# Wider padded tiles in a two-block layer kernel: 576 columns in place of 542

## The chip, the cores and the metric

The kernel runs on one core of one Trainium2 chip. The metric is the device time of one execution in microseconds (us). The kernel before takes 1970.71 us, the median of 3 runs (1970.65 to 1971.37).

## The reference, cut to what matters

The input is a sequence of 512 tokens with 1024 channels. It passes through two blocks of two layers each.

Each layer of the first block normalizes, projects to 3584 channels and splits them into four mixers of 256 channels: (a) a gated 31-wide depthwise convolution with a layer norm, (b) a 3-wide gated convolution, (c) attention in a sliding window, (d) attention in a 2-D neighbourhood. Their gated outputs are joined and projected back.

```python
y_a = conformer_conv(...) * silu(a_z)          # 31-wide convolution over positions
y_b = short_gated_conv(...) * silu(b_z)        # 3-wide convolution
return x + einsum("bse,ed->bsd", concat([y_a, y_b, y_c, y_d]), w_out)
```

Each layer of the second block has a running mean over windows of 2, 4, 8 and 16 tokens, a latent attention with 8 heads, a linear recurrence after a 4-wide convolution, three gates that merge them, an output projection, and a feed-forward part of 4096 hidden channels:

```python
x = x + merged @ w_out
x = x + square(relu(rms_norm(x) @ w_ff1)) @ w_ff2
```

All of it is in 32-bit floats. The kernel multiplies in a split form: each operand is a high part plus a low part, and three products (high by high, high by low, low by high) are summed.

## The kernel before, in words

Activations lie with channels on the 128 partitions and the 512 tokens along the free dimension, so a tile of 128 channels is 128x512 floats, 2048 bytes in each partition. `gemm` (L158 on) makes one such output tile: it loads 512 KB of weights into `raw`, splits them into `whi` and `wlo` (`weights`, L136 to L144, `split`, L122 to L129), and `mm3` (L148 to L154) issues for each of the 8 input tiles three matmuls: `whi` with the high part (L152), `whi` with the low part (L153), `wlo` with the high part (L154). That is 24 matmuls of 128x512 for a tile; the loaded weights are the stationary operand, the activations are streamed.

The second block's layer ends with three stretches made of nothing but such tiles. The output projection (L878 on, `w_out_2`) streams the tiles `mh`, `ml`. Four quarters of the feed-forward part follow; each has 8 tiles with `w_ff1_2` (L894, streaming `hh`, `hl`) and 8 tiles with `w_ff2_2` (L904, streaming `fh`, `fl`). So each of these stretches has 192 matmuls. In the last quarter of the last layer the second product is done otherwise (from L923): there `fh` and `fl` are the stationary operand, the weights `wfh`, `wfl` are streamed, and each of 8 output tiles has 24 matmuls behind four transposes.

All buffers come from pools with a fixed number of slots under a tag. The tiles of one tag lie side by side in each partition, and the tags stand in the order of their first use. The pool `act` has, among others, the tags `hl` (32 slots: the split activations `xh`, `xl`, `hh`, `hl`, `yh`, `oh`, `wfh` and so on), `work` (8), `pad` (3), `hc` (2: the sums of the 31-wide convolution, later two tiles of `v`), `prob` (2), `gate` (16: `fh`, `fl`, `mh`, `ml`, the attention's `q`, `k`, `dq`, `dk`, `dv`, biases and gates) and `pth` (4: `pt`). In the program before, each slot's start is a multiple of 32 bytes, and the starts are these (bytes in each partition):

| tag | first slot at | from slot to slot | bytes of a tile |
|---|---|---|---|
| `raw`, `whi`, `wlo` (weights) | 27008, 35200, 47488 | 4096 | 4096 |
| `hl` | 76160 | 2048 | 2048 |
| `work` | 141696 | 2048 | 2048 |
| `pad` | 164992 | 2176 | 2168 |
| `hc` | 171520 | 2048 | 2048 |
| `prob` | 175616 | 5120 | 5120 |
| `gate` | 185856 | 2048 | 2048 |
| `pth` | 218624 | 2048 | 2048 |

The last byte in use is 226815; a partition has 229376. `c_ident`, the identity of the transposes, is at 18272, `ones_r` at 17760.

The tag `pad` serves the padded inputs of the convolutions (L483, L549), of the running means (L757, L766) and of the recurrence's convolution (L789), and three tiles without padding (`a2`, L810, and `gf`, L918, both cut to 512 columns). GpSimd writes the zeros at their ends. Only L485 writes up to the tile's end: `G.memset(pad[:, S + 15 :], 0.0)`. All others name their columns.

The order of the instructions on each engine is set ahead of time by the planner of the tile framework, which moves work within an engine's queue where its operands and slots allow; the waits follow from the tiles.

Of the kernel before, what the change touches and what calls it, by code (L numbers as in the profile page):

```python
# [9 lines left out]
F32 = mybir.dt.float32  # L10
# [6 lines left out]
P = 128  # L17
S = 512
# [39 lines left out]
def two_blocks(ctx: ExitStack, tc: tile.TileContext, g: dict):  # L58
# [5 lines left out]
    ap_ = ctx.enter_context(tc.tile_pool(name="act", bufs=1))  # L64
# [4 lines left out]
    def uniq(n):  # L69
        cnt[0] += 1  # L70
        return f"{n}_{cnt[0]}"

    def work(n="w", shape=(P, S), dt=F32):
        return ap_.tile(list(shape), dt, tag="work", name=uniq(n), bufs=WORK)
# [13 lines left out]
    def auxps(n="aux"):  # L88
        return ps.tile([P, S], F32, tag="t", name=uniq(n), bufs=2)
# [16 lines left out]
    def col(name, l, c):  # L106
        o, w = VCOL[name]
        o += l * w + c
        return vec[:, o : o + 1]
# [21 lines left out]
    def split_tile(src, scale=None, n="h"):  # L131
        hi, lo = hl(n + "h"), hl(n + "l")
        split(src, hi, lo, scale)
        return hi, lo
# [192 lines left out]
    def scaled(p, R, n="e", alloc=work):  # L327
        t = alloc(n)
        V.tensor_tensor(t, p, R, op=ALU.mult)  # L329
        return t  # L330
# [25 lines left out]
    def hcol(name, l, c):  # L356
        o, w = VCOL[name]
        o += l * w + c
        return hvec[:, o : o + 1]
# [26 lines left out]
    for l in range(DEPTH):  # L386
        def proj(c):
            return first.pop(c) if c in first else gemm(g["w_in"][l, c], xs)
# [72 lines left out]
        for c in range(2):  # L461
            t, r = ts[c], work("cqr")
            rope(t, cos, sin, r, acopy)
            cq.append(queries(r, hl, "cqx"))
        t = scaled(proj(CK), R, "ck")
# [8 lines left out]
        def tap(acc, pad, c, k):  # L474
            V.scalar_tensor_tensor(acc, pad[:, k : k + S], hcol("conv_a_w", l, c * 31 + k), acc,
                                   op0=ALU.mult, op1=ALU.add)

        for c in range(2):
            v = scaled(proj(AV + c), R, "av")
            t = work("avt")  # L480
            A.activation(t, v, AF.Tanh, scale=0.5)
            u = scaled(proj(AU + c), R, "au")
            pad = ap_.tile([P, S + 30], F32, tag="pad", name=uniq("pad"), bufs=3)  # L483
            G.memset(pad[:, :15], 0.0)
            G.memset(pad[:, S + 15 :], 0.0)  # L485
            V.scalar_tensor_tensor(pad[:, 15 : S + 15], t, 1.0, u, op0=ALU.add, op1=ALU.mult)
            acc = ap_.tile([P, S], F32, tag="hc", name=uniq("hc"), bufs=2)
            V.tensor_scalar(acc, pad[:, 0:S], hcol("conv_a_w", l, c * 31), col("conv_a_b", l, c),
                            op0=ALU.mult, op1=ALU.add)
            for k in range(1, 31):  # L490
                taps.append(lambda acc=acc, pad=pad, c=c, k=k: tap(acc, pad, c, k))
            hc.append(acc)
# [53 lines left out]
        def conv_b(c):  # L546
            xb = scaled(proj(BX + c), R, "bx")
            cb = scaled(proj(BC + c), R, "bc")
            pad = ap_.tile([P, S + 30], F32, tag="pad", name=uniq("padb"), bufs=3)  # L549
            G.memset(pad[:, :1], 0.0)  # L550
            G.memset(pad[:, S + 1 : S + 2], 0.0)
            V.tensor_tensor(pad[:, 1 : S + 1], cb, xb, op=ALU.mult)
            return pad
# [36 lines left out]
        def finish_a(c):  # L590
# [10 lines left out]
            "dv": lambda c: values(scaled_tiles(proj(DV + c), "dv"), gate, "dv"),  # L601
            "zd": lambda c: gated(proj(DZ + c), R),
            "xb": conv_b, "hb": gate_b, "yb": finish_b, "ya": finish_a, "ln": lambda c: layer_norm(),
        }
        order = ["zc0", "bias0", "dq0", "zc1", "dk0", "dv0", "xb0", "hb0", "yb0", "zd0", "bias1", "dq1", "dk1", "dv1", "ln0",
# [67 lines left out]
    for l in range(DEPTH):  # L673
# [13 lines left out]
        for c in range(2):  # L687
            t = scaled(proj(5 + c), R, "kl")
# [4 lines left out]
        for c in range(3):  # L693
            t = scaled(proj(2 + c), R, "ql")
# [59 lines left out]
        ypool = {}  # L754

        def pool(c):
            pu = ap_.tile([P, S + 30], F32, tag="pad", name=uniq("padp"), bufs=3)  # L757
            G.memset(pu[:, :16], 0.0)
            V.tensor_tensor(pu[:, 16 : S + 16], proj(c), R, op=ALU.mult)
            cur = pu  # L760
            mixed = work("mixed")

            w = 1
            wins = (2, 4) if c == 0 else (8, 16)
            while w < wins[1]:
                nxt = ap_.tile([P, S + 30], F32, tag="pad", name=uniq("padd"), bufs=3)  # L766
                G.memset(nxt[:, :16], 0.0)
                V.tensor_tensor(nxt[:, 16 : S + 16], cur[:, 16 : S + 16], cur[:, 16 - w : S + 16 - w], op=ALU.add)
                cur = nxt
                w *= 2  # L770
                for j in range(2):
                    if w == wins[j]:
                        r0 = 64 * j
                        V.tensor_tensor(mixed[r0 : r0 + 64, 0:16], cur[r0 : r0 + 64, 16:32], invc[r0 : r0 + 64, c, :],
                                        op=ALU.mult)
                        V.tensor_scalar(mixed[r0 : r0 + 64, 16:], cur[r0 : r0 + 64, 32 : S + 16], 1.0 / w, None,
                                        op0=ALU.mult)
            V.tensor_tensor(mixed, mixed, pu[:, 16 : S + 16], op=ALU.subtract)
            p = auxps("pool")
            T.matmul(p, lhsT=bd["w_pool_grp_2", c], rhs=mixed, start=True, stop=True)  # L780
            t = work("yp")
            A.activation(t, p, AF.Copy, scale=col("pool_scale_2", l, c))
            ypool[c] = split_tile(t, None, "yp")
# [2 lines left out]
        ylru, lru = {}, {}  # L786

        def lru_in(c):
            pu = ap_.tile([P, S + 30], F32, tag="pad", name=uniq("padl"), bufs=3)  # L789
            G.memset(pu[:, :3], 0.0)  # L790
            V.tensor_tensor(pu[:, 3 : S + 3], proj(8 + c), R, op=ALU.mult)
            u = work("u")
            V.tensor_scalar(u, pu[:, 0:S], col("conv_w_2", l, c * 4), col("conv_b_2", l, c), op0=ALU.mult, op1=ALU.add)
            for k in range(1, 4):
                V.scalar_tensor_tensor(u, pu[:, k : k + S], col("conv_w_2", l, c * 4 + k), u, op0=ALU.mult, op1=ALU.add)
            p = auxps("ga")
            T.matmul(p, lhsT=bd["w_lru_a_2", c], rhs=u, start=True, stop=True)
            tr = work("tr")
            A.activation(tr, p, AF.Tanh, bias=hcol("b_lru_a_2", l, c), scale=0.5)
            p = auxps("gx")  # L800
            T.matmul(p, lhsT=bd["w_lru_x_2", c], rhs=u, start=True, stop=True)
            ti = work("ti")
            A.activation(ti, p, AF.Tanh, bias=hcol("b_lru_x_2", l, c), scale=0.5)
            V.scalar_tensor_tensor(ti, ti, 1.0, u, op0=ALU.add, op1=ALU.mult)

            V.tensor_scalar(tr, tr, 1.0, sp4[:, 2 * l + c : 2 * l + c + 1], op0=ALU.add, op1=ALU.mult)
            a = work("a")
            A.activation(a, tr, AF.Exp, scale=-1.0)
            A.activation(tr, tr, AF.Tanh)
            a2 = ap_.tile([P, S + 30], F32, tag="pad", name=uniq("a2"), bufs=3)[:, :S]  # L810
            A.activation(a2, a, AF.Square)
            V.scalar_tensor_tensor(a2, a2, 1.0, tr, op0=ALU.add, op1=ALU.mult)
            lru[c] = (a, a2, ti)
# [20 lines left out]
        def early_gate(m):  # L834
            tg1[m] = gate_of(1, m, gate)

        pieces = [(("pool", c), lambda c=c: pool(c)) for c in range(2)] + [(("lru", c), lambda c=c: lru_in(c)) for c in range(2)]
        pieces += [(("scan", 0), lru_scan)]
        pieces += [(("gate", m), lambda m=m: early_gate(m)) for m in range(KD)]
# [19 lines left out]
        for m in range(KD):  # L859
# [3 lines left out]
            for i, k0, ops_ in ((0, 0, ypool), (2, 6, ylru), (1, 2, yo)):  # L863
                p = mmps("br")
                mm3(p, [((h[:, k0 + k, :], lo[:, k0 + k, :]), ops_[k]) for k in range(len(ops_))])
                t = work("mgt")
# [24 lines left out]
        for qt in range(4):  # L891
            f = []
            for c in range(8):
                p = gemm(g["w_ff1_2"][l, 8 * qt + c], hs)  # L894
                t = work("relu")
# [7 lines left out]
            for m in range(KD):  # L903
                p = gemm(g["w_ff2_2"][l, qt, m], f)  # L904
                t = work("ff")
# [9 lines left out]

    gf = []
    for h in range(2):
        t = ap_.tile([P, S + 30], F32, tag="pad", name=uniq("gf"), bufs=3)[:, :S]  # L918
        nc.sync.dma_start(out=t, in_=g["g_final"][:, h * S : (h + 1) * S].to_broadcast([P, S]))
        gf.append(t)  # L920
    ss = small("ssh")
# [143 lines left out]
```

## Time and profile before

| | |
|---|---|
| median of 3 runs | 1970.71 us |
| the profiled execution | 1971.46 us |
| its span, from the first to the last instruction | 1969.6 us |
| TensorE busy | 1930.3 us, 98% of the span |
| VectorE, ScalarE, GpSimd busy | 1208.8, 839.6, 68.3 us |
| mean granted TensorE clock | 0.996 of full speed (2.4 GHz) |

The profiled execution is one more execution than those of the median. Matmuls are pipelined, so the duration that is shown for one (some 390 ns) is longer than the distance from its start to the start of the next.

### The profile page before, as it was taken

To read this page: it belongs to the slowest core of one execution; us is meant where nothing else is said; L and a number is where in the kernel's file an instruction comes from. 1 tells how busy PE (TensorE), PEld (TensorE's weight loads), DVE (VectorE), ACT (ScalarE), POOL (GpSimd) and SP (SyncE) were. 2 spreads that over 40 slices of the span, in tenths; PEclk is the share of its full clock that TensorE was granted. 3 is DMA by queue.
4 is the path that set the end of the run, shared out by engine and by line. 5 is a ranking of instruction groups with operands and counts; after the bars stand their busy time and mean duration, and the time that the engine had idled before them with its cause. 6 is when DMAs were issued, how large, how long until landed. Compare 5 with 4: busy or idle time off the path is not lost.

```text
span 1969.6 us, 23167 instructions
## 1 busy us (share of the span) xinstructions
PE 1930.3 (98%) x8866; PEld 1532.7 (78%) x8866; DVE 1208.8 (61%) x2127; ACT 839.6 (43%) x1391; POOL 68.3 (3%) x83
## 2 busy tenths in 40 slices
PE   7999999999999999999999999999999999999998
PEld 6777777777776778888888888766788888888886
DVE  8996678966787545565444446786455564444454
ACT  6565354663457633333232324367433333323242
POOL 0000110000200000020000001000000010000001
PEclk9999999999999999999999999999999999999999
DMA  5222222222212123233333333222222323323341
GB/s 191 75 94 84 86 97 75 85 85 66 84 50 79 65 75 97 97 96 93 91 95 96 97 96 97 83 62 83 65 86 97 97 95 91 96 94 97 96 128 43
DMA packets 53678, 175.21 MB, mean 89 GB/s; under 512 B 6208, under 2 KB 10176, under 8 KB 53568
## 3 DMA queue, kind: packets, MB, share of 16 engines
q1 hardware_dynamic: 53568, 173.74, 28.0%
q8 instruction: 70, 1.15, 0.2%
q14 instruction: 40, 0.33, 0.1%
HBM read 171.62 MB, written 2.10 MB: 88 GB/s over the span
## 4 chain that ended last, share of the span: by engine, by line
PE 72%; DVE 3%; ACT 2%; issue 1%; ACTq 0%; DVEq 0%
PE mm L152 20%; PE mm L154 19%; PE mm L153 19%; PE o L313 2%; PE sc L742 2%; PE br L154 1%; PE br L153 1%; PE br L152 1%; PE t L235 1%; PE last L154 1%; PE last L152 1%; PE last L153 1%; DVE wlo L126 1%; ACT p L284 0%; PE ss L169 0%
## 5 line engine op out<-in xcount | busy, mean ns | idle before, releaser
L125 ACT ACTIVATE whi<-raw 128x1024 fp32r<-128x1024 f32 (+2 forms) x314 | 321.4, 1025 | 779.6 <-PE mm L153 577.1
L126 DVE TENSOR_TENSOR wlo<-raw,whi 128x1024 fp32r<-128x1024 f32 (+2 forms) x314 | 369.1, 1176 | 168.1 <-ACT whi L125 168.1
L152 PE MATMUL mm<-xh,whi 128*128 128x512 f32 x992 | 397.8, 401 | 9.0 <-ACT whi L125 8.0
L154 PE MATMUL mm<-xh,wlo 128*128 128x512 f32 x992 | 392.7, 396 | 2.3 <-DVE wlo L126 2.2
L153 PE MATMUL mm<-xl,whi 128*128 128x512 f32 x992 | 394.3, 397 | 0.0
L152 PEld LDWEIGHTS mm<-xh,whi 128*128 128x128 f32 x992 | 187.6, 189 | 50.2 <-ACT whi L125 8.9
L154 PEld LDWEIGHTS mm<-xh,wlo 128*128 128x128 f32 x992 | 187.5, 189 | 43.4 <-DVE wlo L126 4.1
L153 PEld LDWEIGHTS mm<-xl,whi 128*128 128x128 f32 x992 | 187.8, 189 | 40.4 <-issue 4.3
L153 PE MATMUL mm<-hl,whi 128*128 128x512 f32 x512 | 199.5, 390 | 0.0
L152 PE MATMUL mm<-hh,whi 128*128 128x512 f32 x512 | 199.3, 389 | 0.0
L154 PE MATMUL mm<-hh,wlo 128*128 128x512 f32 x512 | 199.2, 389 | 0.0
L154 PE MATMUL mm<-fh,wlo 128*128 128x512 f32 x448 | 177.0, 395 | 0.0
L152 PE MATMUL mm<-fh,whi 128*128 128x512 f32 x448 | 176.9, 395 | 0.0
L153 PE MATMUL mm<-fl,whi 128*128 128x512 f32 x448 | 176.9, 395 | 0.0
L906 DVE TENSOR_TENSOR ff<-mm,rstd 128x512 f32<-128x512 f32 x56 | 38.8, 692 | 148.3 <-PE mm L154 148.3
L152 PEld LDWEIGHTS mm<-hh,whi 128*128 128x128 f32 x512 | 96.1, 188 | 20.1
L153 PEld LDWEIGHTS mm<-hl,whi 128*128 128x128 f32 x512 | 96.1, 188 | 19.9
L154 PEld LDWEIGHTS mm<-hh,wlo 128*128 128x128 f32 x512 | 96.1, 188 | 19.9
L329 DVE TENSOR_TENSOR lg<-mm,rstd 128x512 f32<-128x512 f32 x48 | 33.2, 691 | 124.3 <-PE mm L154 124.2
L154 PEld LDWEIGHTS mm<-fh,wlo 128*128 128x128 f32 x448 | 84.1, 188 | 20.4
L153 PEld LDWEIGHTS mm<-fl,whi 128*128 128x128 f32 x448 | 84.1, 188 | 20.4
L152 PEld LDWEIGHTS mm<-fh,whi 128*128 128x128 f32 x448 | 84.1, 188 | 20.4
(302 smaller groups left out, 2801.0 us busy)
## 6 DMA issues: line engine op xcount, KB each, us to landing
raw<-in_w_in SPq DMA_DIRECT2D x124, 512.0 KB, 3.3
raw<-in_w_ff SPq DMA_DIRECT2D x120, 512.0 KB, 3.6
raw<-in_w_out SPq DMA_DIRECT2D x32, 512.0 KB, 3.5
raw<-in_w_br SPq DMA_DIRECT2D x16, 512.0 KB, 3.6
raw<-in_w_last SPq DMA_DIRECT2D x8, 512.0 KB, 3.6
raw<-in_w_q SPq DMA_DIRECT2D x12, 192.0 KB, 2.3
x<-in_xT SPq DMA_DIRECT2D x8, 256.0 KB, 6.5
bends<-in_rpb SPq DMA_DIRECT2D x8, 256.0 KB, 4.4
```

What stands on the lines that cost most here:

```text
L125: A.activation(hi, src, AF.Copy)
L126: V.tensor_tensor(lo, src, hi.bitcast(F32), op=ALU.subtract)
L152: T.matmul(out, lhsT=wh, rhs=xh, start=(first and i == 0), stop=False)
L153: T.matmul(out, lhsT=wh, rhs=xl, start=False, stop=False)
L154: T.matmul(out, lhsT=wl, rhs=xh, start=False, stop=(last and i == n - 1))
L235: T.matmul(out, lhsT=in_, rhs=ident, is_transpose=True, start=True, stop=True)
L313: T.matmul(out[64 * j : 64 * j + 64, i * P : (i + 1) * P], lhsT=v(b), rhs=pts[j][:, (b - b0) * P : (b - b0 + 1) * P], start=(b == b0), sto ...
L329: V.tensor_tensor(t, p, R, op=ALU.mult)
L742: T.matmul(out, lhsT=q[h][:, i * P : (i + 1) * P], rhs=kt[h][:, b0 * P : b1 * P], start=True, stop=True)
L906: V.tensor_tensor(t, p, Rf2, op=ALU.mult)
```

## The change

Every tile of the tag `pad` becomes 576 columns wide in place of 542, in eight places of the code. No line is added or taken away. Each tile has 2304 bytes in place of 2168, and what comes behind the three slots in the partition begins further up. The slice `pad[:, S + 15 :]` of L485 now has 49 columns in place of 15.

```diff
-            pad = ap_.tile([P, S + 30], F32, tag="pad", name=uniq("pad"), bufs=3)
+            pad = ap_.tile([P, S + 64], F32, tag="pad", name=uniq("pad"), bufs=3)
             G.memset(pad[:, :15], 0.0)
             G.memset(pad[:, S + 15 :], 0.0)
...
-            pad = ap_.tile([P, S + 30], F32, tag="pad", name=uniq("padb"), bufs=3)
+            pad = ap_.tile([P, S + 64], F32, tag="pad", name=uniq("padb"), bufs=3)
...
-            pu = ap_.tile([P, S + 30], F32, tag="pad", name=uniq("padp"), bufs=3)
+            pu = ap_.tile([P, S + 64], F32, tag="pad", name=uniq("padp"), bufs=3)
...
-                nxt = ap_.tile([P, S + 30], F32, tag="pad", name=uniq("padd"), bufs=3)
+                nxt = ap_.tile([P, S + 64], F32, tag="pad", name=uniq("padd"), bufs=3)
...
-            a2 = ap_.tile([P, S + 30], F32, tag="pad", name=uniq("a2"), bufs=3)[:, :S]
+            a2 = ap_.tile([P, S + 64], F32, tag="pad", name=uniq("a2"), bufs=3)[:, :S]
...
-        t = ap_.tile([P, S + 30], F32, tag="pad", name=uniq("gf"), bufs=3)[:, :S]
+        t = ap_.tile([P, S + 64], F32, tag="pad", name=uniq("gf"), bufs=3)[:, :S]
```

(`padl`, L789, changes in the same way.)

## Rows read from the trace of the kernel before

**Rows 1.** The page, busy time, share of the span and instructions of two engines.
```profile
PE 1930.3 (98%) x8866; PEld 1532.7 (78%) x8866; DVE 1208.8 (61%) x2127; ACT 839.6 (43%) x1391; POOL 68.3 (3%) x83
PEclk9999999999999999999999999999999999999999
```
**Rows 2.** The page, chain that ended last: share of the span by engine.
```profile
PE 72%; DVE 3%; ACT 2%; issue 1%; ACTq 0%; DVEq 0%
```
**Rows 3.** Groups by line and shape, TensorE; columns: count, busy us, mean ns, idle before.
```profile
L152 PE MATMUL mm<-hh,whi 128*128 128x512 f32 x512 | 199.3, 389 | 0.0
L154 PE MATMUL mm<-hh,wlo 128*128 128x512 f32 x512 | 199.2, 389 | 0.0
L154 PE MATMUL mm<-fh,wlo 128*128 128x512 f32 x448 | 177.0, 395 | 0.0
L152 PE MATMUL mm<-fh,whi 128*128 128x512 f32 x448 | 176.9, 395 | 0.0
...
L152 PE MATMUL mm<-mh,whi 128*128 128x512 f32 x128 | 50.6, 395 | 0.0
...
L152 PE MATMUL last<-wfh,fh 128*128 128x512 f32 x64 | 25.9, 405 | 0.0
L154 PE MATMUL last<-wfh,fl 128*128 128x512 f32 x64 | 25.3, 395 | 0.0
...
L152 PE MATMUL br<-oh,whi 128*128 128x512 f32 x64 | 24.9, 389 | 0.0
```
**Rows 4.** Timeline of TensorE: starts (us) where one stretch gives way to the next.
```profile
840.63 0.40 PE L152 MATMUL mm<-mh,whi 128*128 128x512 f32 x1
...
885.43 0.39 PE L152 MATMUL mm<-hh,whi 128*128 128x512 f32 x1
...
975.58 0.39 PE L152 MATMUL mm<-hh,whi 128*128 128x512 f32 x1
...
1019.11 0.40 PE L152 MATMUL mm<-fh,whi 128*128 128x512 f32 x1
...
1063.90 0.39 PE L152 MATMUL mm<-hh,whi 128*128 128x512 f32 x1
```
**Rows 5.** Windows of ff1 and ff2: PE, PEld, DVE, ACT, POOL, clock, DMA, GB/s.
```profile
976.00:1018.00 42.00, 42.00 (x187) 34.74 (x186) 19.92 (x24) 15.89 (x22) 0.00 (x0) 1.00 0.31 94
1020.00:1062.00 42.00, 42.00 (x181) 33.79 (x180) 20.17 (x24) 8.76 (x10) 0.00 (x0) 1.00 0.28 88
```
**Rows 6.** Waits inside the same ff2 stretch: us in total, times, longest.
```profile
ACT whi L125 <- PE mm L153: 31.0, 8, 4.5
DVE ff L906 <- PE mm L154: 19.7, 7, 3.0
```
**Rows 7.** Groups by line and shape: score matmuls from two tags.
```profile
L437 PE MATMUL sc<-dk,dq 128*128 128x384 f32 x32 | 8.8, 345 | 0.0
L437 PE MATMUL sc<-ckx,cqx 128*128 128x384 f32 x32 | 8.4, 345 | 0.0
```
**Rows 8.** Groups by line and shape: matmuls on `ones_r`, `pt` and the values.
```profile
L313 PE MATMUL o<-pt,v 128*64 128x128 f32 x320 | 35.9, 286 | 2.5 <-ACT pt L309 2.2
L313 PE MATMUL o<-pt,cv 128*64 128x128 f32 x160 | 18.8, 288 | 0.4
L313 PE MATMUL o<-pt,dv 128*64 128x128 f32 x160 | 18.6, 287 | 0.0
...
L201 PE MATMUL sp<-dl,ones_r 128*128 128x512 f32 x15 | 6.1, 408 | 0.0
```
**Rows 9.** Groups by line and shape on GpSimd: the memsets of 16, 15 and 3 columns.
```profile
L767 POOL MEMSET padd<- 128x16 f32 x12 | 1.3, 111 | 134.4 <-DVE convb L560 49.8 <-DVE hc L475 32.3 <-DVE padd L768 31.7
...
L485 POOL MEMSET pad<- 128x15 f32 x4 | 0.4, 111 | 0.0
L790 POOL MEMSET padl<- 128x3 f32 x4 | 0.4, 100 | 7.1 <-DVE mixed L778 3.7 <-DVE padd L768 3.4
```
**Rows 10.** Instructions on `pad`: ns min/median/max, first and last start us.
```profile
L475 DVE SCALAR_TENSOR_TENSOR hc<-pad,hvec,hc x120: 723/749/762, 51.9 to 399.2; 128x512 f32<-128x512 f32 x120
L485 POOL MEMSET pad<- x4: 111/111/112, 0.8 to 149.5; 128x15 f32 x4
L486 DVE SCALAR_TENSOR_TENSOR pad<-avt,au x4: 689/691/693, 49.6 to 311.9; 128x512 f32<-128x512 f32 x4
```

More of the change, by code (lines that the diff above doesn't have):

```diff
@@ L788, in lru_in @@
         def lru_in(c):
-            pu = ap_.tile([P, S + 30], F32, tag="pad", name=uniq("padl"), bufs=3)
+            pu = ap_.tile([P, S + 64], F32, tag="pad", name=uniq("padl"), bufs=3)
             G.memset(pu[:, :3], 0.0)
```

## The prediction

> **What bounds the kernel now.** I read the page first. TensorE is busy for 1930.3 us, 98% of the span, at the full granted clock (its 2.4 GHz level) in every slice [rows 1], and the chain that ended last runs through TensorE for 72% of the span, through VectorE for 3% and ScalarE for 2% [rows 2]. So what counts is how many matmuls there are and how far apart they start; work on the other engines counts only where a matmul waits for it.
>
> I then asked whether equal matmuls take equal time, because an edit that moves addresses can act only there. The groups by line and shape [rows 3] hold the same instruction, 128x512 on 128x128 weights, several times over. Streaming `hh` or `oh` (tag `hl`) it takes a mean of 389 ns; streaming `fh` or `mh` (tag `gate`) 395 ns; with `fh` stationary and `wfh` (tag `hl`) streamed 395 to 405 ns. No group shows idle time. The timeline gives the distance of starts [rows 4]. A ff1 stretch of 192 matmuls runs from 975.58 to 1019.11, 43.53 us or 226.7 ns each; the ff2 stretch right behind it, also of 192, from 1019.11 to 1063.90, 44.79 us or 233.3 ns each. The output projection, again 192, runs from 840.63 to 885.43, 44.80 us. So 192 matmuls on `gate` tiles cost 1.26 us more than 192 on `hl` tiles.
>
> That is not a shortage. In a ff2 stretch TensorE is busy for all of the window, with the clock at 1.00, VectorE is busy for 20.17 of 42 us, as in ff1 (19.92), ScalarE for less than in ff1 (8.76 against 15.89), and DMA takes no more [rows 5]. VectorE and ScalarE wait for TensorE there, up to 3.0 and 4.5 us at a time [rows 6].
>
> **Where the tiles lie.** The table of slots gives addresses; I take them modulo 512 bytes, the length of one 128-column weight slice, since the slices of `whi` and `wlo` step by just that. Weights (35200, 47488): 384. `hl` (76160): 384. `gate` (185856): 0. A matmul on `hl` tiles thus has a streamed operand and weights at one residue, whichever slice and slot; a matmul on `gate` tiles has them 128 bytes apart. The last stretch, with `fh` stationary and `wfh` streamed, has the same 128 bytes with the roles exchanged, and it is as slow. Score matmuls on `dk`, `dq`, both in `gate` and so at one residue, take 345 ns like those on `ckx`, `cqx` in `hl` [rows 7]. So it is not that `gate` lies high in the partition; the distance between the two operands decides.
>
> **The change part by part.** The edit gives each `pad` slot 2304 bytes. Before, a tile of 2168 bytes stands in a slot of 2176, since starts are multiples of 32; 2304 is such a multiple. The tags behind therefore move by 3 x (2304 - 2176) = 384 bytes, not by the 3 x 136 = 408 that the tile widths alone suggest. The residue of `gate` becomes 0 + 384 = 384, that of the weights and of `hl`. Weights, `hl` and `work` lie before `pad` and stay.
>
> First term: ff2. `fh` has 448 matmuls in each of L152 and L154 [rows 3], with as many on `fl`: 1344, or 7 stretches of 192. Second term: the output projection with `mh`, `ml`, 3 x 128 = 384, or 2 stretches. These 9 stretches save 1.26 us each if they go at the distance of ff1: 11.3 us. Third term: the last stretch, 3 x 64 = 192 matmuls, the same excess: 1.26 us less about nothing for its transposes; I take 1.2. The sum is 12.5 us. Its cover: none is needed, for these stretches are TensorE from end to end. What would be late next is the weights' split, and ff1 shows a TensorE that never waits at 226.7 ns with the heavier load on ScalarE [rows 5].
>
> Other operands that move. `hc`, `prob`, `gate` and `pth` go together, so `dk` with `dq`, `k` with `q`, and `pt` with `dv` keep their distance. `pt` against `cv` and against the part of `v` in `hl` changes (residues 0 and 384 now, equal after); `o` takes 286 to 288 ns whichever value tile it has [rows 8]. I take 0, with 640 matmuls by 2 ns, 1.3 us, to either side; the 320 transposes of `p` move against `c_ident` as well, and at the same 2 ns add 0.6.
>
> VectorE's 120 taps read `pad` and update `hc`, which move against each other. They take 723 to 762 ns, median 749 [rows 10]: all at the one end saves 3.1 us of VectorE, all at the other costs 1.6. VectorE makes up 3% of the chain [rows 2]; I take 0, and both ends for the range.
>
> The four memsets of L485 grow from 15 to 49 columns. Between 3 and 15 columns the time grows from 100 to 111 ns, 0.92 ns a column [rows 9], so they become 111 + 34 x 0.92 = 142 ns, 0.12 us in all. The last start at 149.5 us, while `pad` is written up to 311.9 [rows 10]; only further memsets queue behind them, and GpSimd is busy for 68.3 us of the span [rows 1]. Cost 0; without the cover, 0.12 us. No instruction, wait or DMA is added. The planner's costs hardly change, so I expect its order to stay.
>
> The profiled execution has 1971.46 us (span 1969.6): 1971.46 - 12.5 = 1958.96. The median of the runs is 0.75 us lower: 1958.2 us. The bounds of the small terms, 3.1 + 1.3 + 0.6 = 5 us down and 3.5 up, could at most give 1953 to 1962; they don't all come together, and for the likeliest case I take 1955.5 to 1961.7.
>
> **A rule that speaks against it.** The two kinds of matmul differ by 6 ns of duration and 6.6 ns of distance at one shape and clock [rows 3, 4]. The Trainium skill, SBUF — State Buffer, section "SBUF: two separate sides", says that engine-side contention is confined to the port pair shared by VectorE and GpSimd and that TensorE never waits for a port. By that rule an address could not matter and the sum would be 0. The rows disagree with it as far as the difference goes; they don't show by themselves what its cause is.
>
> **The rivals.**
>
> - *The excess is not from the distance of operands* but from something that the `gate` stretches share, such as the place in the partition. Nothing then changes: 1970.7. For it: that `fh` and `mh` never occur at another residue before. Against it: the change of pace at 1019.11 and back at 1063.90, stretches with different companions (the output projection and ff2), the last stretch, and the scores.
> - *The distance matters, but in part*: some finer or coarser pattern (1024 bytes, slot against slot) leaves half of the excess. 1970.7 - 6.3 = 1964.4. Against it: `hl` tiles meet weight slices at all steps of 512 and all go at 389 ns.
> - *The move is 408 bytes after all*. Then `gate` lies 24 bytes from the weights' residue. The nearest row is `sp` (L201), whose `ones_r` has residue 352, 32 bytes from `dl` in `work` (384): 408 ns, 13 ns over the 395 of now [rows 8]. At its worst that is 1920 x 13 ns = 25 us: 1995.7. It decides where the mean of `fh` matmuls rises over 395 ns; any mechanism with a worse distance after than before would show there. Against it: slots of 2176 bytes for tiles of 2168.
>
> **How the numbers follow.** The forecast has 0.80, the partial gain 0.06, no change 0.09, the slower case 0.05. The range reaches from the low end of the forecast over the partial case, 1955.5 to 1966, and leaves out the last two (0.14). A measurement of this kernel tells about 0.2%, 3.9 us, from no change: the first two cases are faster (0.86), the third is the same (0.09), the last is slower (0.05).
>
> **What would show it.** In the profile after, `fh`, `mh` and `last` take 389 to 390 ns (the first of a `last` group more), and a ff2 stretch 43.5 us like ff1; `hh` is unchanged; L485 takes about 142 ns; the counts are the same. If `fh` stays at 395 ns the first rival holds; if it lies between, the second; above, the third. If `fh` falls to 389 and the time does not follow by 11 to 13 us, a wait that I left out took the gain.

## The result, and the profile after

The kernel after takes 1958.95 us, the median of 6 runs (1957.22 to 1960.24), against 1971.53 us of 6 runs of the kernel before beside it (1970.65 to 1973.55). The ratio is 0.9935, 95% interval 0.9925 to 0.9945: 12.6 us or 0.65% faster, and the forecast was 1958.2 us.

The page of the kernel after, busy time and granted clock, answers to [rows 1]. TensorE has as many instructions as before and 11.7 us less busy time, at the same clock; VectorE and GpSimd have what they had.

```profile
PE 1918.6 (98%) x8866; PEld 1533.4 (78%) x8866; DVE 1208.8 (62%) x2127; ACT 837.7 (43%) x1391; POOL 68.3 (3%) x83
...
PEclk9999999999999999999999999999999999999999
```

The groups by line and shape of the kernel after (count, busy us, mean ns, idle before) answer to [rows 3]. `fh` and `mh` went from 395 to 389 ns, the time of `hh` and `oh`, which stayed; `last` fell by 4 ns in both lines shown.

```profile
L152 PE MATMUL mm<-hh,whi 128*128 128x512 f32 x512 | 199.2, 389 | 0.0
...
L152 PE MATMUL mm<-fh,whi 128*128 128x512 f32 x448 | 174.3, 389 | 0.0
...
L154 PE MATMUL mm<-fh,wlo 128*128 128x512 f32 x448 | 174.3, 389 | 0.0
...
L152 PE MATMUL mm<-mh,whi 128*128 128x512 f32 x128 | 49.8, 389 | 0.0
...
L152 PE MATMUL last<-wfh,fh 128*128 128x512 f32 x64 | 25.7, 401 | 0.0
L154 PE MATMUL last<-wfh,fl 128*128 128x512 f32 x64 | 25.0, 391 | 0.0
...
L152 PE MATMUL br<-oh,whi 128*128 128x512 f32 x64 | 24.9, 389 | 0.0
```

The timeline of TensorE in the kernel after, at the boundaries of [rows 4]. The output projection takes 885.17 - 841.65 = 43.52 us, ff1 1017.54 - 974.02 = 43.52, ff2 1061.06 - 1017.54 = 43.52. All three kinds of stretch have become equal, 226.67 ns from start to start; before, two of the three took 44.8.

```profile
841.65 0.39 PE L152 MATMUL mm<-mh,whi 128*128 128x512 f32 x1
...
885.17 0.39 PE L152 MATMUL mm<-hh,whi 128*128 128x512 f32 x1
...
974.02 0.39 PE L152 MATMUL mm<-hh,whi 128*128 128x512 f32 x1
...
1017.54 0.39 PE L152 MATMUL mm<-fh,whi 128*128 128x512 f32 x1
...
1061.06 0.39 PE L152 MATMUL mm<-hh,whi 128*128 128x512 f32 x1
```

One difference between the two profiles goes the other way. The first matmul on `mh` starts at 841.65 us, 1.02 later than before, and from there to the end of the span it is 1116.55 us against 1128.97, 12.4 less; so the span fell by 11.4 us only. In the profiles of the twelve kernels of this study whose `hl` tiles and weights stand to each other as before, that start lies between 838.79 and 841.65; the kernel after has the latest. With one profile of each kernel it isn't shown whether the change has a part in this 1 us.

The small things of [rows 10] in the kernel after (ns min/median/max), and two score and value groups that answer to [rows 7, 8]:

```profile
L475 DVE SCALAR_TENSOR_TENSOR hc<-pad,hvec,hc x120: 720/747/756, 51.7 to 400.3; 128x512 f32<-128x512 f32 x120
...
L485 POOL MEMSET pad<- x4: 138/138/139, 0.8 to 149.1; 128x49 f32 x4
```

```profile
L313 PE MATMUL o<-pt,cv 128*64 128x128 f32 x160 | 18.8, 288 | 0.4
...
L437 PE MATMUL sc<-dk,dq 128*128 128x384 f32 x32 | 8.7, 342 | 0.0
L437 PE MATMUL sc<-ckx,cqx 128*128 128x384 f32 x32 | 8.5, 345 | 0.0
```

### The profile page after: what moved, and what is told of

Read it like the earlier page. It is cut to its first block, busy times and chain, and to the rows that moved or that the text cites. A ratio compares the mean times of both kernels' runs of the same rounds, so it can differ in the third digit from the quotient of the medians.

```text
span 1958.2 us, 23167 instructions
## 1 busy us (share of the span) xinstructions
PE 1918.6 (98%) x8866; PEld 1533.4 (78%) x8866; DVE 1208.8 (62%) x2127; ACT 837.7 (43%) x1391; POOL 68.3 (3%) x83
## 4 chain that ended last, share of the span: by engine, by line
PE 72%; DVE 3%; ACT 2%; issue 1%; ACTq 0%; DVEq 0%
PE mm L152 20%; PE mm L153 19%; PE mm L154 19%; PE o L313 2%; PE sc L742 2%; PE br L153 1%; PE br L152 1%; PE br L154 1%; PE t L235 1%; PE last L154 1%; PE last L152 1%; PE last L153 1%; DVE wlo L126 1%; PE ss L169 0%; DVE x L626 0%
## 5 line engine op out<-in xcount | busy, mean ns | idle before, releaser
L152 PE MATMUL mm<-xh,whi 128*128 128x512 f32 x992 | 398.2, 402 | 9.4 <-ACT whi L125 8.4
L154 PE MATMUL mm<-xh,wlo 128*128 128x512 f32 x992 | 392.8, 396 | 2.3 <-DVE wlo L126 2.2
L153 PE MATMUL mm<-xl,whi 128*128 128x512 f32 x992 | 394.7, 398 | 0.0
L152 PEld LDWEIGHTS mm<-xh,whi 128*128 128x128 f32 x992 | 187.9, 189 | 50.7 <-ACT whi L125 9.2
L154 PEld LDWEIGHTS mm<-xh,wlo 128*128 128x128 f32 x992 | 187.8, 189 | 43.6 <-DVE wlo L126 4.1
L153 PEld LDWEIGHTS mm<-xl,whi 128*128 128x128 f32 x992 | 188.0, 189 | 40.2 <-issue 4.3
L153 PE MATMUL mm<-hl,whi 128*128 128x512 f32 x512 | 199.4, 389 | 0.0
L152 PE MATMUL mm<-hh,whi 128*128 128x512 f32 x512 | 199.2, 389 | 0.0
L154 PE MATMUL mm<-hh,wlo 128*128 128x512 f32 x512 | 199.2, 389 | 0.0
L152 PE MATMUL mm<-fh,whi 128*128 128x512 f32 x448 | 174.3, 389 | 0.0
L153 PE MATMUL mm<-fl,whi 128*128 128x512 f32 x448 | 174.3, 389 | 0.0
L154 PE MATMUL mm<-fh,wlo 128*128 128x512 f32 x448 | 174.3, 389 | 0.0
L152 PEld LDWEIGHTS mm<-hh,whi 128*128 128x128 f32 x512 | 96.1, 188 | 20.1
L154 PEld LDWEIGHTS mm<-hh,wlo 128*128 128x128 f32 x512 | 96.1, 188 | 19.8
L153 PEld LDWEIGHTS mm<-hl,whi 128*128 128x128 f32 x512 | 96.1, 188 | 19.8
L152 PEld LDWEIGHTS mm<-fh,whi 128*128 128x128 f32 x448 | 84.1, 188 | 17.6
L154 PEld LDWEIGHTS mm<-fh,wlo 128*128 128x128 f32 x448 | 84.1, 188 | 17.4
L153 PEld LDWEIGHTS mm<-fl,whi 128*128 128x128 f32 x448 | 84.1, 188 | 17.3
```

The costliest lines, as they stand in the source:

```text
L152: T.matmul(out, lhsT=wh, rhs=xh, start=(first and i == 0), stop=False)
L153: T.matmul(out, lhsT=wh, rhs=xl, start=False, stop=False)
L154: T.matmul(out, lhsT=wl, rhs=xh, start=False, stop=(last and i == n - 1))
```

## The experiments

In what follows a distance is the address of the `gate` tiles minus that of the weights, modulo 256 bytes unless said otherwise. The order of the instructions on each engine was that of the kernels before and after in all of them, apart from one memset that *wlo_off_128* adds on GpSimd. The runs of the kernel before beside them have medians of 1970.7 to 1972.0 us.

### Is it the distance of operands? Four runs

*gate_back* is the kernel after with only `gate` and `pth` put back to their old residue.

```diff
-            self.p = ap_.tile([P, 10 * P], F32, tag="prob", name=uniq("p"), bufs=PROBS)
+            self.p = ap_.tile([P, 10 * P + 16], F32, tag="prob", name=uniq("p"), bufs=PROBS)
...
-                pair = ap_.tile([P, 10 * P], F32, tag="prob", name=uniq("yh"), bufs=PROBS)
+                pair = ap_.tile([P, 10 * P + 16], F32, tag="prob", name=uniq("yh"), bufs=PROBS)
```

> The changed kernel with the two prob slots 64 bytes longer each, so that gate (and pt) goes 128 bytes further, back to residue 0 modulo 512, while pad, hc and prob keep their new places (the second prob slot moves by 64). Theory A (the distance between gate tiles and weights modulo 512 costs TensorE 6.6 ns per matmul): ff2 and output-projection stretches go back to 44.8 us per 192 matmuls, ff1 stays at 43.5, the time is that of the kernel before, 1971.5 us. Rival B (the gain came from pad, hc or prob lying elsewhere, or from the wider memsets): it stays at 1959 us and 43.5 us.

Measured: 1971.14 us, ratio to before 1.0000 (0.9990 to 1.0009). The whole gain is gone although `pad`, `hc` and `prob` keep their new places and the memset its new length. The timeline of this kernel has its ff2 stretch at 1063.51 - 1018.71 = 44.80 us again, and ff1 at 43.53.

```profile
975.18 0.39 PE L152 MATMUL mm<-hh,whi 128*128 128x512 f32 x1
...
1018.71 0.40 PE L152 MATMUL mm<-fh,whi 128*128 128x512 f32 x1
...
1063.51 0.39 PE L152 MATMUL mm<-hh,whi 128*128 128x512 f32 x1
```

*all_up_128* is the kernel before with weights, `hl` and `gate` moved by 128 bytes together.

```diff
-    ones = cst.tile([P, 1], F32, name="ones")
+    ones = cst.tile([P, 33], F32, name="ones")[:, :1]
```

> The kernel before with one constant 128 bytes longer, so that the weights, hl, work, pad, hc, prob, gate and pt all move up by 128 bytes: weights and hl at residue 0, gate at residue 128. Theory A (the distance between the two operands): nothing changes, 1971.5 us, ff1 43.5 us and ff2 44.8 us per 192 matmuls. Rival C (a tile whose own start is a multiple of 512 is slow, whatever the weights): now the hl tiles are the slow ones, ff1 44.8 us, and 5484 matmuls on hl tiles pay up to 6.6 ns each, up to 36 us more.

Measured: 1972.06 us, ratio 1.0001 (0.9992 to 1.0010); ff2 44.79 us. An operand's own place doesn't matter, at least for this step.

*weights_up_128* is the kernel before with only the weights moved by 128 bytes.

```diff
-    x = [ap_.tile([P, S], F32, tag=f"x{k}", name=f"x{k}", bufs=1) for k in range(KD)]
+    x = [ap_.tile([P, S + 96 * (k == 0)], F32, tag=f"x{k}", name=f"x{k}", bufs=1)[:, :S] for k in range(KD)]
...
-    ones = cst.tile([P, 1], F32, name="ones")
+    ones = cst.tile([P, 33], F32, name="ones")[:, :1]
```

> The kernel before with only the weights moved in residue (up 128, to 0); hl, work, hc and gate move by a whole 512 bytes and keep their residues 384, 384, 0 and 0. Theory A: the two kinds exchange places: ff2 and output projection 43.5 us per 192, ff1 44.8 us; 1728 matmuls save 11.3 us, 1920 in ff1 and in the branch projections (hh, br) lose 12.6 us, and up to 3564 more on hl tiles lose up to 23 us where TensorE is the limit: between 1972 and 1996 us, I take 1988. Rival C (the streamed tile's own address): nothing changes, 1971.5 us.

Measured: 1981.41 us, ratio 1.0052 (1.0037 to 1.0067). The two kinds change places, as its groups show against [rows 3], and the last stretch, which uses none of the moved weights, is as slow as before:

```profile
L152 PE MATMUL mm<-xh,whi 128*128 128x512 f32 x992 | 402.0, 406 | 9.0 <-ACT whi L125 8.1 <-DVE cq L329 0.9
...
L152 PE MATMUL mm<-hh,whi 128*128 128x512 f32 x512 | 202.2, 395 | 0.0
...
L152 PE MATMUL mm<-fh,whi 128*128 128x512 f32 x448 | 174.3, 389 | 0.0
...
L152 PE MATMUL last<-wfh,fh 128*128 128x512 f32 x64 | 25.9, 405 | 0.0
```

The sign was as expected, the size was not: +10.1 us against an expected 17. In the trace of before, `xh` on `whi` takes 401 ns, so here it is up by 5, not by 6.6, and these products share their stretches with other work; that this is why the size was off was not tested by itself.

*gate_up_256* is the kernel before with `gate` 256 bytes further up (both `prob` tiles `10 * P + 32`, edited as in *gate_back*), so that it lies 128 bytes below the weights modulo 512, not above.

> The kernel before with the two prob slots 128 bytes longer each: gate and pt move up by 256 bytes, to residue 256, 128 bytes below the weights' residue, where before they lie 128 above it. Theory A with the same cost on both sides: 44.8 us per 192, 1971.5 us. If the cost follows a pattern that is not symmetric, a distance between 43.5 and more than 44.8 us; if only multiples of 512 are slow for gate (rival C), 43.5 us and 1959 us.

Measured: 1971.83 us, ratio 1.0002 (0.9992 to 1.0012); ff2 takes 44.79 us, from 1019.30 to 1064.09.

### Which distances cost? Six runs

Five kernels are the kernel before with wider `prob` tiles, by the columns named below, in one of them with wider `pad` tiles too. *gate_fan* is the kernel before and gives the slots of `gate` 2080 bytes, so that successive slots lie 32 bytes further on each:

```diff
-        return ap_.tile(list(shape), dt, tag="gate", name=uniq(n), bufs=16)
+        return ap_.tile([P, S + 8], dt, tag="gate", name=uniq(n), bufs=16)[:, :S]
```

*gate_up_128* (`10 * P + 16`):

> The kernel before with gate and pt up by 128 bytes (the two prob slots 64 bytes longer each): gate at residue 128, a distance of 256 bytes from the weights' residue. Since distances of 128 to either side cost 233.3 ns a matmul and all multiples of 512 cost 226.7, the pattern repeats every 512 or every 256 bytes. If every 256: ff2 43.5 us per 192 matmuls and 1959 us; if every 512: 44.8 us and 1971.5 us. I expect 512.

*gate_up_448* (`10 * P + 56`):

> The kernel before with gate and pt up by 448 bytes: gate at residue 448, 64 bytes above the weights' residue. If only an equal residue is fast: 44.8 us per 192 matmuls and 1971.5 us. If the cost grows with the distance up to 128: about half of it, 44.1 us and 1965 us.

*gate_up_416* (`10 * P + 40`, and `S + 38` for `S + 30` in the seven lines that allocate `pad` tiles; the change itself touches seven lines too, not eight):

> The kernel before with gate and pt up by 416 bytes: gate at residue 416, 32 bytes above the weights' residue, the least step of a slot and near the 408 bytes that the tile widths alone suggest. If only an equal residue is fast: 44.8 us per 192 matmuls and 1971.5 us. If the cost grows with the distance: a quarter of it, 43.8 us and 1962 us. By the matmuls on ones_r, which lie 32 bytes off, it would be slower than before: up to 1995 us.

*gate_fan*:

> The kernel before with every gate tile in a slot of 2080 bytes, so that the 16 slots have the residues 0, 32, 64 and so on to 480. If a matmul's cost depends on its own distance and only an equal residue is fast: 15 of 16 tiles at 233.3 ns and one at 226.7, ff2 44.7 us per 192 matmuls and about 1971 us. If it falls off with the distance, the tiles in the slots near residue 384 are faster than the others, and the stretch lies between 43.5 and 44.8 us.

*gate_up_320* (`10 * P + 40`):

> The kernel before with 40 columns more in each prob tile, all else as before: gate, and pth behind it, begin 320 bytes further up, the streamed tiles of gate at residue 320 modulo 512, 64 bytes below the weights' 384. Theory: the pattern repeats every 256 bytes and is the same to both sides, so that 64 bytes below costs what 64 bytes above did (gate_up_448: ff2 at 228.97 ns from start to start, 1963.5 us): 192 starts in 43.9 to 44.0 us, about 1963.5 us. Rival 1: the side counts, and 64 below (which modulo 256 is 192 above) costs another amount, 230 to 233.3 ns a matmul: 1966 to 1971.5 us. Rival 2: below costs nothing: 226.7 ns, 1959.5 us.

*gate_up_64* (`10 * P + 8`):

> The kernel before with 8 columns more in each prob tile: gate at residue 64 modulo 512, 320 bytes below the weights' 384, which modulo 256 is 64 below, as in gate_up_320. Theory of a period of 256 bytes: the same ff2 distance as gate_up_320, within 0.3 ns a matmul, and the same time within 1.5 us; if both sides are alike as well, 228.9 ns and 1963.5 us. Rival (a period of 512, with which the 1959.7 us of gate_up_128 at 256 bytes is only a second good spot): another distance than gate_up_320, most likely the 233.3 ns of before, 1971.5 us.

The stretches are differences of starts in each kernel's timeline, of the ff2 stretch at about 1018 us:

| kernel | residue of `gate` mod 512 | distance mod 256 | ff2, us | ns from start to start | time, us | ratio to before (interval) |
|---|---|---|---|---|---|---|
| after | 384 | 0 | 43.52 | 226.7 | 1958.95 | 0.9935 (0.9925 to 0.9945) |
| *gate_up_128* | 128 | 0 | 43.52 | 226.7 | 1959.66 | 0.9940 (0.9925 to 0.9954) |
| *gate_up_416* | 416 | 32 | 44.80 | 233.3 | 1970.94 | 0.9995 (0.9985 to 1.0004) |
| *gate_up_448* | 448 | 64 | 43.96 | 229.0 | 1963.52 | 0.9960 (0.9945 to 0.9975) |
| before | 0 | 128 | 44.79 | 233.3 | 1971.53 | |
| *gate_up_256* | 256 | 128 | 44.79 | 233.3 | 1971.83 | 1.0002 (0.9992 to 1.0012) |
| *gate_up_64* | 64 | 192 | 44.79 | 233.3 | 1970.62 | 0.9995 (0.9986 to 1.0005) |
| *gate_up_320* | 320 | 192 | 44.80 | 233.3 | 1970.03 | 0.9993 (0.9984 to 1.0003) |
| *gate_fan* | all steps of 32 | mixed | 44.49 | 231.7 | 1967.38 (one run) | |

Timeline of *gate_up_128* and of *gate_up_448*, the ff2 stretch of each:

```profile
1017.15 0.39 PE L152 MATMUL mm<-fh,whi 128*128 128x512 f32 x1
...
1060.67 0.39 PE L152 MATMUL mm<-hh,whi 128*128 128x512 f32 x1
```

```profile
1016.42 0.40 PE L152 MATMUL mm<-fh,whi 128*128 128x512 f32 x1
...
1060.38 0.40 PE L152 MATMUL mm<-hh,whi 128*128 128x512 f32 x1
```

Three of these expectations fell. I had taken 512 bytes for the period; *gate_up_128*, 256 bytes from the weights, is as fast as the kernel after, and each of the two other pairs of residues that were tried 256 bytes apart (0 with 256, 64 with 320) gives one and the same stretch. These two pairs say little alone, for 233.3 ns is what most residues give, and the rival of *gate_up_64* named that value too. But 256 bytes account for all that was seen. Second, the cost doesn't grow with the distance: 32 bytes cost all of it, 64 bytes a third. Third, the two sides are not alike: 64 above costs 2.3 ns a matmul, 64 below (192) 6.6. Only five of the eight steps of 32 were tried alone. *gate_fan* has all eight at once: 16 tiles in 16 slots, two at each distance. Its nine stretches on `gate` tiles take 44.45 to 44.60 us, 44.53 in the mean. An estimate from the other rows, with 6.6 ns for 96, 160 and 224 as well, is (0 + 2.3 + 6 x 6.6) / 8 = 5.24 ns a matmul, 44.53 us a stretch. So those three may well cost the full 6.6 ns, but *gate_fan*, whose neighbouring tiles lie at different distances, doesn't show them one by one.

Which side is the cheap one depends on which operand is streamed, as the last stretch shows: there `wfh`, `wfl` are streamed and the `gate` tiles are the weights. From its first to its last matmul it takes 46.75 us in the kernel after and 47.65 before, 47.72 (1952.16 - 1904.44) in *gate_up_448*, but 46.99 in both *gate_up_64* and *gate_up_320*, whose `gate` tiles lie 64 below. So what counts is the streamed tile's address minus that of the weights, and 64 above is cheap in either arrangement. That 46.99 comes back at residues 64 and 320 also speaks for the 256 bytes better than the full cost of ff2 does. Groups of *gate_up_64*:

```profile
L152 PE MATMUL last<-wfh,fh 128*128 128x512 f32 x64 | 25.9, 405 | 0.0
...
L154 PE MATMUL last<-wfh,fl 128*128 128x512 f32 x64 | 25.1, 392 | 0.0
...
L153 PE MATMUL last<-wfl,fh 128*128 128x512 f32 x64 | 24.9, 389 | 0.0
```

A note on reading: in *gate_up_448* the three groups of ff2 differ: `fh` on `whi` takes 394 ns, `fl` on `whi` 388 and `fh` on `wlo` 392, where the kernel after has 389 in all three. One line alone misleads; the mean of the three, 391.3, is 2.3 above 389, as the starts have it. All costs here are such means: in the kernel before nearly all distances from start to start in ff2 are, by turns, 229 to 230 and 237 to 238 ns, of which 233.3 is the mean, while in *gate_up_64* all are 233 or 234.

```profile
L152 PE MATMUL mm<-fh,whi 128*128 128x512 f32 x448 | 176.5, 394 | 0.0
...
L154 PE MATMUL mm<-fh,wlo 128*128 128x512 f32 x448 | 175.6, 392 | 0.0
L153 PE MATMUL mm<-fl,whi 128*128 128x512 f32 x448 | 173.9, 388 | 0.0
```

### Which two reads collide? Two runs

*wlo_off_128* is the kernel after with only `wlo` displaced: 128 bytes between the slots of `whi` and `wlo`, and `x0` widened so that the rest moves by 512.

```diff
-    x = [ap_.tile([P, S], F32, tag=f"x{k}", name=f"x{k}", bufs=1) for k in range(KD)]
+    x = [ap_.tile([P, S + 96 * (k == 0)], F32, tag=f"x{k}", name=f"x{k}", bufs=1)[:, :S] for k in range(KD)]
...
-        lo = wp.tile([P, CH], F32R, tag="wlo", name=uniq("wlo"), bufs=WBUF)
+        len(cnt) > 1 or (cnt.append(0), G.memset(wp.tile([P, 32], F32, tag="gap", name="gap", bufs=1), 0.0)); lo = wp.tile([P, CH], F32R, tag="wlo", name=uniq("wlo"), bufs=WBUF)
```

> The kernel after, with 128 bytes put between the slots of whi and those of wlo, and x0 96 columns wider so that everything from there on moves by 512 in all: whi, hl and gate have the residues they have after (384), wlo has 0. One memset of 32 columns is added on GpSimd at the start. So of the three matmuls of mm3 (whi high L152, whi low L153, wlo high L154) only the load of wlo is 128 bytes off, in each stretch. Theory 1 (a matmul is stretched while the weights of the next one are read beside its streamed tile): only the start-to-start time from L153 to L154 grows, by about 6.6 ns on average over a stretch, to 233; L152 and L154 stay at 226.7. Theory 2 (the matmul's own weights): only from L154 to the next L152. Either way a ff1 or ff2 stretch takes 64 x 6.6 = 0.42 us more than 43.52 us, 43.95, and 24-matmul tiles in all, some 2400 matmuls on wlo, at most 16 us: 1967 to 1975 us. Theory 3 (the cost needs an unbroken run of displaced pairs): no change, 1959 us.

Measured: 1980.95 us, ratio 1.0047 (1.0032 to 1.0062), 22.0 us over the kernel after and beyond the 16 that I had as the most. Neither of the two theories of one stretched matmul held: a ff1 stretch takes 1023.02 - 978.65 = 44.37 us, 0.85 more than 43.52, or 13.3 ns for each group of three. The starts of that ff1 stretch, taken over its 192 matmuls, lie 226.7 ns apart from L152 to L153, 232.7 from L153 to L154 and 234.0 from L154 to L152: two of three are stretched, by 6.0 and 7.3, near the usual 6.6. Groups and timeline of this kernel (PEld is the load of the weights for the line named; one load runs beside each matmul):

```profile
L153 PE MATMUL mm<-hl,whi 128*128 128x512 f32 x512 | 202.9, 396 | 0.0
...
L152 PE MATMUL mm<-hh,whi 128*128 128x512 f32 x512 | 199.2, 389 | 0.0
...
L154 PE MATMUL mm<-hh,wlo 128*128 128x512 f32 x512 | 203.2, 397 | 0.0
```

```profile
990.43 0.39 PE L152 MATMUL mm<-hh,whi 128*128 128x512 f32 x1
990.44 0.19 PEld L153 LDWEIGHTS mm<-hl,whi 128*128 128x128 f32 x1
990.66 0.40 PE L153 MATMUL mm<-hl,whi 128*128 128x512 f32 x1
990.66 0.19 PEld L154 LDWEIGHTS mm<-hh,wlo 128*128 128x128 f32 x1
...
990.89 0.40 PE L154 MATMUL mm<-hh,wlo 128*128 128x512 f32 x1
990.89 0.19 PEld L152 LDWEIGHTS mm<-hh,whi 128*128 128x128 f32 x1
991.13 0.39 PE L152 MATMUL mm<-hh,whi 128*128 128x512 f32 x1
```

The displaced load of `wlo` is shown beside L153, yet L154, beside which `whi` is loaded at distance 0, is stretched as well. Either a load meets two streamed tiles, or a stretched matmul drags the next along. The counterpart tells these apart.

*lo_off_128* is the kernel after with all weights in place and only the streamed low parts `fl` and `ml` displaced by 128 bytes; `OFF` holds the numbers of the tiles that begin 128 bytes into their slot. Slots of 2176 bytes lie by turns 0 and 128 bytes off modulo 256 by themselves, so `OFF` names low parts in some slots and high parts in others; modulo 256 the high parts come to a distance of 0 and the low parts to 128. The other tiles of `gate` lie as their slots fall.

```diff
-        return ap_.tile(list(shape), dt, tag="gate", name=uniq(n), bufs=16)
+        t = ap_.tile([P, S + 32], dt, tag="gate", name=uniq(n), bufs=16); o = 32 * (cnt[0] in OFF); return t[:, o : o + S]
```

> The counterpart of wlo_off_128, in which one displaced load in three stretched two of three starts: here all loads of weights keep residue 384, and of the streamed tiles only the low parts fl and ml (L153) lie 128 bytes off; fh, mh keep 384. It is the kernel after with gate slots of 2176 bytes, and in each slot the tile begins 0 or 128 bytes in, by the kind of tile. Theory 1 (a load is read during the time of two matmuls, that before its own and its own, and stretches each whose streamed tile is displaced against it, by some 6.6 ns however many loads it meets): only L153 to L154 grows, to about 233.3 ns; a ff2 stretch takes 43.52 + 64 x 6.6 ns = 43.95 us, the output projection too, and the kernel 1959 + 9 x 0.42 + about 0.4 = 1963 us. Theory 2 (what is read beside a displaced operand stretches its own matmul and the next one): L153 to L154 and L154 to L152 grow, a ff2 stretch takes 44.37 us, the kernel 1967 us. Theory 3 (only displaced loads cost): no change, 43.52 and 1959 us.

Measured: 1962.39 us, ratio 0.9957 (0.9941 to 0.9974), 3.4 us over the kernel after, where theory 1 has 4 and theory 2 has 8. The output projection and ff2 take 43.95 us each (883.94 - 839.99, 1060.68 - 1016.73). Only L153 is stretched; from start to start this ff2 stretch has 226.7 ns behind L152, 234.3 behind L153 and 225.7 behind L154:

```profile
L153 PE MATMUL mm<-fl,whi 128*128 128x512 f32 x448 | 177.0, 395 | 0.0
L152 PE MATMUL mm<-fh,whi 128*128 128x512 f32 x448 | 174.3, 389 | 0.0
L154 PE MATMUL mm<-fh,wlo 128*128 128x512 f32 x448 | 173.8, 388 | 0.0
```

```profile
839.99 0.39 PE L152 MATMUL mm<-mh,whi 128*128 128x512 f32 x1
...
883.94 0.39 PE L152 MATMUL mm<-hh,whi 128*128 128x512 f32 x1
...
1016.73 0.39 PE L152 MATMUL mm<-fh,whi 128*128 128x512 f32 x1
...
1060.68 0.39 PE L152 MATMUL mm<-hh,whi 128*128 128x512 f32 x1
```

So a stretched matmul doesn't drag the next along: here it would have. The last stretch of the same kernel has the roles exchanged and agrees: there the displaced `fl` is the load of L154, one in three, and both L153 (395 against 390 ns in the kernel after) and L154 (396 against 391) are stretched, L152 hardly (402 against 401).

```profile
L152 PE MATMUL last<-wfh,fh 128*128 128x512 f32 x64 | 25.7, 402 | 0.0
...
L154 PE MATMUL last<-wfh,fl 128*128 128x512 f32 x64 | 25.4, 396 | 0.0
...
L153 PE MATMUL last<-wfl,fh 128*128 128x512 f32 x64 | 25.3, 395 | 0.0
```

A matmul is stretched where its streamed tile lies displaced against its own weights or against the next ones, once, and not twice where both are displaced (in the kernel before both are, and the mean cost is 6.6 ns). That fits a load that is read during two matmuls. What in the chip lets the two reads disturb each other isn't shown; the runs show only that the difference of the addresses, which 256 bytes repeat, decides.

No long stretch of any kernel went below 226.67 ns in the mean from start to start, and at a distance of 0 all have 226.7 to 227.0, so the runs point to no version that beats the kernel after.

## Why the prediction was right

- **The bound.** TensorE was the bound, and the gain came at once and in full: 12.4 us from the first matmul on `mh` to the end.
- **The distance decides.** *gate_back*, *all_up_128* and *weights_up_128* show it, one by undoing it alone, one by moving both operands, one by moving the other operand. The first rival (a property of the `gate` stretches) fell with them. By the rule that the prediction set against itself (the Trainium skill, SBUF — State Buffer, "SBUF: two separate sides": TensorE never waits for a port) the sum would have been 0; the measured 12.6 us decide against that here.
- **The move is 384 bytes.** The kernel after shows it: `gate` at 384 bytes further up lies on the weights' residue, and `fh` fell to 389 ns. 408 bytes would have left 24. The third rival fell, and its price was wrong as well: 32 bytes off (*gate_up_416*) cost the 6.6 ns of before and no more, 1970.94 us, not 1995.7. `sp`, from which that price was taken, has 410 ns in the kernel after, with its distance as it was; 32 bytes cost 6.6 ns of that where they were tried, and what else makes it slow isn't shown.
- **The terms.** The nine stretches were put at 1.26 us each, 11.3 us; the output projection and ff2 measured 1.28 and 1.27. The last stretch was put at 1.2: from the first to the last of its matmuls it fell from 47.65 to 46.75 us, 0.90. This is the one term that was too large. The gain there is 4 to 5 ns a matmul, as the groups show, not 6.6.
- **The modulus.** 512 bytes, taken from the length of a slice, was too coarse: 256 suffices. Nothing in the trace before could tell, for its long stretches had only the distances 0 and 128. The answer for 384 bytes is the same by either. The same goes for the second rival, a gain in part: a finer pattern exists (*gate_up_448* at 1963.52 us is just such a case), but the change landed on a distance of 0, the best that was tried.
- **What was taken as 0.** The values' products stayed at 288 ns [rows 8]. VectorE's taps went from 749 to 747 ns median, 0.24 us in all, against bounds of 3.1 down and 1.6 up. The memset of 49 columns takes 138 ns, not 142, and nothing waited for it; the prediction's remark that only further memsets queue behind it was wrong, for GpSimd also runs 38 sums of squares (L223), but the next of them starts 84 us behind the last L485. The score matmuls on `dk`, `dq`, which I had left out, fell from 345 to 342 ns, 0.1 us in all; they keep their distance to each other, all fourteen kernels of this study have 342 to 345, and why they differ is open.

## What to carry to other kernels

Where one shape of matmul takes two times in one profile, group by the tag of the streamed tile and compare its address with that of the weights modulo 256 bytes, before looking for a wait: 6.6 ns in 233 cost this kernel 0.65%, with the same instructions in the same order on every engine. Any edit that changes a tile's width moves all tags behind it, by the slots' width, rounded up to a multiple of 32 bytes here, and can win or lose this much without touching the code that pays for it; so pad pools on purpose, and move one tag at a time when you test it.

## What was not expected of the hardware

- The distance of a streamed tile to the weights counts modulo 256 bytes, and not evenly: 226.7 ns at 0, 233.3 at 32, 229.0 at 64, 233.3 at 128 and 192 (means over 192 matmuls; the streamed tile's address minus that of the weights).
- With an operand 128 bytes off, one displaced load in three stretches two matmuls in three (44.37 us a stretch), one displaced streamed tile in three only one (43.95 us).
